# Two-layer hybrid transformer block on one core: the first norm's modulations as float32 matmuls, both conditions at once

## The chip, the cores and the metric

The kernel runs on one core of a Trainium2 chip. The metric is device time in microseconds (us) of one execution; the time of a kernel is the median of its runs.

A core has TensorE (in the profile PE, and PEld for its weight loads), VectorE (DVE), ScalarE (ACT), GpSimd (POOL), and SyncE (SP), whose queue issues most of the loads here. Each engine takes its own instructions in the order in which they were compiled. The "granted clock" is the share of TensorE's full clock that the chip allowed in a stretch of time.

## The reference

Two streams go through two layers: 512 latent tokens `x` and 256 context tokens `ctx`, each 1024 wide. In each layer a conditioning vector (`c` for the latents, `c_ctx` for the context) gives six vectors of 1024, the modulations. Cut to what matters here:

```python
def rms_norm(x, g):
    y = xf * lax.rsqrt(jnp.mean(xf * xf, axis=-1, keepdims=True) + EPS)
    return y * g

def adaln(cond, w_mod, b_mod):
    return jnp.split(jax.nn.silu(cond) @ w_mod + b_mod, N_MOD, axis=-1)

for l in range(DEPTH):
    sh1, sc1, gt1, sh2, sc2, gt2 = adaln(c, w_mod[l], b_mod[l])
    csh1, csc1, cgt1, csh2, csc2, cgt2 = adaln(c_ctx, w_mod[l], b_mod[l])
    h_ctx = rms_norm(ctx, norm1[l]) * (1 + csc1) + csh1
    h = rms_norm(x, norm1[l]) * (1 + sc1) + sh1
    p = h @ w_in[l]          # q, k, v, the convolution branch, the spatial gate, three gates
    ...                      # attention, two other branches, merge, output projection
    x = x + gt1 * merged
    x = x + gt2 * swiglu(rms_norm(x, norm2[l]) * (1 + sc2) + sh2)
```

The change concerns `sh1`, `sc1`, `csh1` and `csc1` of layer 0: 2048 columns of `w_mod[0]` (1024 rows each), multiplied with two vectors.

## The kernel before

**Layout and arithmetic.** Activations lie with the feature on the partition: eight column tiles (k = 0 to 7) of 128 features by 768 tokens, 512 latent ones and then 256 of the context. A matrix product splits each operand into two float32r parts, a high part (ScalarE casts, line 201) and the rest (GpSimd or VectorE subtracts, line 202), and makes three passes on TensorE per 128x128 weight tile (line 211): high by high, high weights by low activations, low weights by high activations. `load_piece` (189) brings in 128x512 weights (tiles `ws`, five buffers) and splits them (`wh`, `wl`, four buffers each).

**Modulations.** `mod_block` (126) makes one 128-feature block of one modulation on VectorE. It loads the block transposed (two halves of 128x512, tiles `wm`, six buffers, line 130), multiplies each half with the Silu of the conditioning vector, which lies broadcast over the partitions in `sbc`, and sums along the row (line 136). Line 139 adds the bias, and line 143 makes `G1`, the norm's gain times one plus the scale. In layer 0 the first norm needs 16 blocks (eight of the scale, eight of the shift).

**The beginning.** The conditioning vector, x in three loads and the first weights are brought in. `norm_stats` (223) sums the squares, reduces them over partitions with float32 matmuls against a column of ones (235), and leaves the reciprocal root in a PSUM tile `RB`. Then, for each column tile k, line 408 on: two `mod_block`s for the latents' condition, `norm_apply` (248: VectorE line 254, ScalarE 256 or 259, and the split into `hh` and `hl`), and 18 passes on TensorE (six weight tiles of `w_six`, three passes each) that add to six open PSUM banks: the latents' k, v and four q projections. `first_stage` (317) lets the first six `wm` loads wait for a copy by GpSimd that reads x.

**After it.** The second condition is loaded to `sbc` (417). `post_k`, `post_v` and `post_q` work on the six banks (head statistics with float32 matmuls at line 295, and a rotation by 32 partitions through DMAs on ScalarE's queue, `rope`, 389). Then come the latents' convolution branch (`branch_a`, 454) and spatial gate (`branch_c`, 492). Amid these steps `ctx_mods` (558) makes the same 16 blocks again, for the context's condition, with the weights read again. After all of them comes the context's norm (568), and then the context's projections, attention, merge, output projection and feed forward. The other modulations are made later by the same `mod_block`, both conditions at once, a block at a time beside the merge and the feed forward (`pump`).

**What sets the order.** The code gives an order in which the program is written; a planner then simulates the engines and places each instruction on its engine when its operands are there, earlier instructions of the program first. Buffers are handed out by the same planner: an instruction that needs a buffer waits for the last reader of its former content. Some loads are held back by hand, with a one-element GpSimd copy into the tile that reads a later activation (lines 322, 416, 420, 426).

Of the kernel before, what the change touches and what calls it, by code (L numbers as in the profile page):

```python
# [16 lines left out]
P = 128  # L17
# [3 lines left out]
KD = 8  # L21
# [3 lines left out]
# columns of the packed small vectors, per layer  # L25
# [7 lines left out]
NPRE = 1  # merge columns whose gates are computed while the attention runs  # L33
# [3 lines left out]
def dit_block(ctx: ExitStack, tc: tile.TileContext, xT, conds, vecs, ident_in, rope_c, rope_s,  # L37
# [5 lines left out]
    PBUFS = {"D": 4, "F": 1, "O": 1, "PT": 2, "st": 1, "RB": 1, "hst": 1, "KB": 1, "VT": 1, "gst": 1,  # L43
# [27 lines left out]
    # four of the eight banks stay with two wide tiles, which the scores and the products take in turn  # L71
# [3 lines left out]
    def banks(n, tag):  # L75
        """n banks for the product of one block."""
        if tag != "D":
            return [pst(tag) for _ in range(n)]
        turn[0] += 1
        if n == 2:  # L80
            i = turn[0] % 3
            return [wide[i][:, 0:512], wide[i][:, 512:1024]] if i < 2 else [pst("D"), pst("D")]
        i = turn[0] % 8
        return [pst("D")] if i % 2 else [wide[i // 4][:, i // 2 % 2 * 512:i // 2 % 2 * 512 + 512]]

    def f(t):
        return t.bitcast(F32)

# [1 line left out]
    # one tile for all that stays  # L90
    fixed = const.tile([P, 3328], F32, name="fixed")
# [12 lines left out]
    sbc = keep(2, 1024)  # L104
    ident = keep(P)
# [49 lines left out]
    def wm_stage():  # L155
        return wp.tile([P, 512], F32, tag="wm", name="wm", bufs=6)
# [47 lines left out]
    def mm(dst, w, acts, segs, k=None):  # L204
        """dst[i][n, tok] (+)= sum_k w[k]^T act[k] for the segments, three passes of the split operands."""
        n = len(acts)
        for kk in ([k] if k is not None else range(n)):
            (wh, wl), (ah, al) = w[0 if k is not None else kk], acts[kk]
            for i, (ww, aa) in enumerate(((wh, ah), (wh, al), (wl, ah))):
                for d, (a, b) in zip(dst, segs):  # L210
                    nc.tensor.matmul(d[:, :b - a], lhsT=ww, rhs=aa[:, a:b], start=kk == 0 and i == 0,  # L211
                                     stop=kk == n - 1 and i == 2)
# [59 lines left out]
    def lagged(gemm_j, full, parts, norm_of, nlag=4):  # L272
        """the first columns whole; the last ones part by part, the norm of one part under the next."""
# [34 lines left out]
    nc.scalar.dma_start(sbc[:, 0, :], conds[0:1, :].to_broadcast([P, 1024]))  # L308
# [5 lines left out]
    nc.scalar.activation(sbc[:, 0, :], sbc[:, 0, :], AF.Silu)  # L314
    n_stage = [0]

    def first_stage():
        """the first of these loads go after most of x."""
        t = wm_stage()
        n_stage[0] += 1  # L320
        if n_stage[0] <= 6:
            nc.gpsimd.tensor_copy(t[:, 0:1], X[NX][:, 0:1])
        return t

    for l in range(2):
# [5 lines left out]
        # ================= tiles of the attention =================  # L331
# [57 lines left out]
        def rope(t):  # L389
            """rotates the latent columns of t in place."""  # L390
# [12 lines left out]
        # ================= norm 1, the first projections =================  # L403
        h = hnext if last else new_h()
        if l == 0:
            six = [wide[0][:, 0:512], wide[0][:, 512:], wide[1][:, 0:512], wide[1][:, 512:], pst("D"), pst("D")]
# [15 lines left out]

        late = h[0 if last else 3][0]  # loads that are not needed at once wait for this
# [26 lines left out]
        # ================= branch a: gated short convolution =================  # L450
# [33 lines left out]
        # ================= branch c: spatial gate =================  # L484
# [66 lines left out]
        def run(*gens):  # L551
            """takes a step of each in turn."""
# [25 lines left out]
        # ================= attention =================  # L578
# [77 lines left out]
        # ================= gated merge =================  # L656
# [44 lines left out]
        # ================= output projection and residual =================  # L701
# [25 lines left out]
        # ================= feed forward =================  # L727
# [49 lines left out]
def _layout(inp):  # L777
    """Host side: layout only (transposes, reorders, copies)."""
# [16 lines left out]
    for l in range(2):  # L795
# [12 lines left out]

    w_modT = a["w_mod"].transpose(0, 2, 1).reshape(2, 48, P, 1024)
# [5 lines left out]
        "xT": xT, "conds": np.stack([a["c"][0], a["c_ctx"]]), "vecs": vecs, "ident": np.eye(P, dtype=f4), "rope_c": rope_c, "rope_s": rope_s,  # L815
# [21 lines left out]
```

## Time and profile before

| | |
|---|---|
| median of 3 runs | 2028.22 us (2025.04 to 2030.04) |
| profiled execution, first to last instruction | 2027.8 us |
| mean granted clock | 0.984 |
| VectorE busy | 1061.6 us (52%) |
| ScalarE, GpSimd busy | 709.3 us (35%), 816.6 us (40%) |
| all bytes read from the chip's memory | 213.53 MB |

The profile lists each engine's instructions with their start and length. In a row such as `L211 PE MATMUL wide<-hh,wh 128*128 128x512 f32`, L211 is the code line, then come engine, operation, the tile written and those read, and the shapes. A row of a timeline begins with the start and the length in us; in brackets behind it stands how long the engine had been idle and what ended that. "SPq" and "ACTq" are issues of DMAs. In a table by stretches each row is a stretch of the execution, its length, and for each engine busy us and number of instructions, then the granted clock, the busy share of the 16 DMA engines and GB/s. Matmuls overlap, so a matmul's length is longer than the distance of two starts; the distance is what counts in a chain. A float32 matmul shows as two load-and-matmul pairs.

### The profile page before, as it was taken

The numbers are of one execution on the slowest core, as the hardware profiler recorded it, in microseconds if no ns is written. First come the engines' busy times: TensorE is split into PE (matmuls) and PEld (weight loads), VectorE is DVE, ScalarE is ACT, GpSimd is POOL, SyncE is SP. The second block draws the span as 40 slices with busy tenths as digits, with TensorE's granted clock in tenths as the row PEclk, the third lists the DMA queues.
The fourth block names the chain that finished last, engine by engine and source line by source line (L and its number), as shares of the span: only waits on it lengthen the run. The fifth ranks groups of instructions, "written<-read, shape, count | busy, mean of one in ns | idle before, by whom it ended". The sixth has DMA issues, their size and how long they took to land.

```text
span 2027.8 us, 28580 instructions
## 1 busy us (share of the span) xinstructions
PE 1931.9 (95%) x10390; PEld 1653.6 (82%) x10390; DVE 1061.6 (52%) x2104; ACT 709.3 (35%) x1361; POOL 816.6 (40%) x702
## 2 busy tenths in 40 slices
PE   5789999998899999999999999999999999999999
PEld 4578998887788788888888888787878888888887
DVE  7977775999999722212221236648733362222222
ACT  3336765212123422212202225447633353223231
POOL 5567644646322422212312226753333343323232
PEclk9899999999899999999999999999999999999999
DMA  8833211545579221221121124330032343333332
GB/s 290 271 109 99 69 32 60 185 151 165 172 244 337 89 63 47 63 79 49 56 89 48 46 73 150 104 104 11 17 104 89 120 135 104 100 98 93 100 100 87
DMA packets 124445, 223.27 MB, mean 110 GB/s; under 512 B 14224, under 2 KB 23184, under 8 KB 124304
## 3 DMA queue, kind: packets, MB, share of 16 engines
q1 hardware_dynamic: 122240, 218.30, 34.1%
q10 hardware_dynamic: 2064, 3.15, 0.5%
q8 instruction: 82, 1.34, 0.3%
q14 instruction: 59, 0.48, 0.1%
HBM read 213.53 MB, written 5.24 MB: 108 GB/s over the span
## 4 chain that ended last, share of the span: by engine, by line
PE 61%; DVE 5%; issue 1%; ACT 1%; DMA 0%; POOL 0%; ACTq 0%; DVEq 0%; POOLq 0%
PE wide L211 34%; PE pD L211 24%; PE pF L211 1%; PE pO L626 1%; DVE junk L136 1%; DVE nm L597 1%; PE pPT L620 1%; DVE nacc L232 0%; PE wide L593 0%; DVE ptl L623 0%; DVE ny L254 0%; ACT pth L622 0%; DVE xr L717 0%; DVE wl L202 0%; DVE qq L398 0%
## 5 line engine op out<-in xcount | busy, mean ns | idle before, releaser
L202 POOL TENSOR_TENSOR wl<-ws,wh 128x512 fp32r<-128x512 f32 (+1 forms) x368 | 497.4, 1358 | 737.2 <-ACT wh L201 540.7
L201 ACT CAST wh<-ws 128x512 fp32r<-128x512 f32 (+1 forms) x560 | 328.3, 608 | 400.0 <-PE wide L211 99.3
L211 PE MATMUL wide<-hh,wh 128*128 128x512 f32 (+1 forms) x1264 | 390.9, 361 | 26.9 <-ACT gate L663 10.1
L211 PE MATMUL wide<-hl,wh 128*128 128x512 f32 (+1 forms) x1264 | 393.9, 362 | 4.3 <-POOL hl L202 3.5
L211 PE MATMUL wide<-hh,wl 128*128 128x512 f32 (+1 forms) x1264 | 389.9, 359 | 2.2 <-POOL wl L202 1.5
L202 DVE TENSOR_TENSOR wl<-ws,wh 128x512 fp32r<-128x512 f32 x192 | 181.7, 946 | 313.3 <-ACT wh L201 290.5
L211 PEld LDWEIGHTS wide<-hh,wh 128*128 128x128 f32 x1264 | 213.6, 192 | 65.8 <-ACT gate L663 11.5
L136 DVE SCALAR_TENSOR_TENSOR junk<-wm,fixed 128x512 f32<-128x512 f32 x320 | 258.5, 818 | 6.7 <-DMA wm<-in_w_modT 4.7
L211 PEld LDWEIGHTS wide<-hl,wh 128*128 128x128 f32 x1264 | 215.0, 192 | 42.0 <-POOL hl L202 5.4
L211 PEld LDWEIGHTS wide<-hh,wl 128*128 128x128 f32 x1264 | 215.2, 192 | 39.4 <-POOL wl L202 1.9
L211 PE MATMUL pD<-hh,wh 128*128 128x512 f32 (+1 forms) x632 | 209.2, 364 | 4.3 <-DVE qq L379 1.5
L211 PE MATMUL pD<-hl,wh 128*128 128x512 f32 (+1 forms) x632 | 212.0, 365 | 0.6 <-POOL hl L202 0.5
L211 PE MATMUL pD<-hh,wl 128*128 128x512 f32 (+1 forms) x632 | 210.4, 363 | 1.7 <-POOL wl L202 1.7
L202 POOL TENSOR_TENSOR ul<-su,uh 128x768 fp32r<-128x768 f32 (+1 forms) x44 | 69.4, 1577 | 199.8 <-ACT uh L201 192.5
L211 PEld LDWEIGHTS pD<-hh,wh 128*128 128x128 f32 x632 | 111.5, 190 | 23.7 <-ACT qa L383 1.9
L211 PEld LDWEIGHTS pD<-hh,wl 128*128 128x128 f32 x632 | 112.6, 190 | 21.7 <-POOL wl L202 2.3
L211 PEld LDWEIGHTS pD<-hl,wh 128*128 128x128 f32 x632 | 112.1, 190 | 19.7 <-POOL hl L202 1.2
L201 ACT CAST uh<-su 128x768 fp32r<-128x768 f32 (+1 forms) x44 | 32.0, 728 | 224.5 <-DVE su L740 224.5
L602 POOL TENSOR_SCALAR pp<-pp,nm 128x768 f32<-128x768 f32 (+1 forms) x80 | 66.9, 838 | 97.8 <-DVE nm L601 67.4
L211 PE MATMUL wide<-ul,wh 128*128 128x512 f32 (+1 forms) x310 | 94.5, 356 | 0.0
L211 PE MATMUL wide<-uh,wl 128*128 128x512 f32 (+1 forms) x310 | 93.6, 352 | 0.0
L211 PE MATMUL wide<-uh,wh 128*128 128x512 f32 (+1 forms) x310 | 93.4, 352 | 0.0
(238 smaller groups left out, 3155.3 us busy)
## 6 DMA issues: line engine op xcount, KB each, us to landing
ws<-in_w SPq DMA_DIRECT2D x244, 256.0 KB, 2.7
wm<-in_w_modT SPq DMA_DIRECT2D x224, 256.0 KB, 4.0
ws<-in_w_in SPq DMA_DIRECT2D x184, 256.0 KB, 3.0
ws<-in_w_o SPq DMA_DIRECT2D x48, 256.0 KB, 4.0
ws<-in_w_abc SPq DMA_DIRECT2D x32, 256.0 KB, 2.8
ws<-in_w SPq DMA_DIRECT2D x36, 192.0 KB, 2.5
ws<-in_w_six SPq DMA_DIRECT2D x16, 192.0 KB, 4.8
xr<-in_xT SPq DMA_DIRECT2D x8, 384.0 KB, 6.4
```

Source lines behind the costliest of these rows:

```text
L136: nc.vector.scalar_tensor_tensor(junk, parts[hh], 1.0, sbc[:, c, hh * 512:(hh + 1) * 512], op0=ALU.mult, op1=ALU.mult, accum_out=acc[:, hh ...
L201: nc.scalar.copy(hi, src)
L202: (lo_eng or nc.gpsimd).tensor_tensor(lo, src, f(hi), op=ALU.subtract)
L211: nc.tensor.matmul(d[:, :b - a], lhsT=ww, rhs=aa[:, a:b], start=kk == 0 and i == 0, stop=kk == n - 1 and i == 2)
L597: nc.vector.tensor_reduce(nm[:, 0:1], D[:, :nk], axis=AX.X, op=ALU.max, negate=True)
L602: nc.gpsimd.tensor_scalar(pt[:, :nk], pt[:, :nk], nm[:, 3:4], 0.0, op0=ALU.mult, op1=ALU.add)
L620: nc.tensor.transpose(TD[:, (2 * j + cc) * P:(2 * j + cc + 1) * P], pts[cc][:, kc:kc + P], ident)
L626: nc.tensor.matmul(o[:, 0:256], lhsT=v3[:, kt, :], rhs=pp[:, j * 256:(j + 1) * 256], start=gi == 0 and j == 0 and i == 0, stop=gi == len(k ...
```

## The change

- The host lays out the scale and shift columns of `w_mod[0]` as `w_m0`, untransposed, with 128x128 blocks that TensorE can take as weights, and both conditions as `condT` (128 partitions, 8 by 2). The kernel loads `condT` first and takes its Silu (16 columns).
- `first_loads(b)` brings in the four 128x512 pieces for column tile b (new tiles `wmt`, 14 buffers). `first_mods(b)` makes scale and shift of both conditions with 16 float32 matmuls of two columns into a new PSUM tile `md`, and VectorE writes `G1` and `MOD` from it with two small operations. `bm1` holds the scale's bias plus one.
- In the loop over k the loads and matmuls of k + 1 stand ahead of the passes of k. The two pieces of `w_six` are loaded together.
- `first_stage`, the latents' 16 `mod_block`s, `ctx_mods` and its loads go. The context's norm takes its steps amid the latents' branches.
- The broadcast conditions in `sbc`, which the later modulations still read, are loaded on ScalarE's queue after the last column's `hh`, and their Silu stands before the attention.

```diff
+    sct = keep(KD, 2)
+    nc.sync.dma_start(sct, condT)
...
-    nc.scalar.dma_start(sbc[:, 0, :], conds[0:1, :].to_broadcast([P, 1024]))
...
-    nc.scalar.activation(sbc[:, 0, :], sbc[:, 0, :], AF.Silu)
-    n_stage = [0]
-
-    def first_stage():
...
+    nc.scalar.activation(sct, sct, AF.Silu)
+    bm1 = keep(KD)
+    nc.vector.tensor_scalar(bm1, vcol(0, V_BM + KD, KD), 1.0, None, op0=ALU.add)
+
+    def first_loads(b):
+
+        parts = []
+        for i in range(2):
+            for hh in range(2):
+                t = wp.tile([P, 512], F32, tag="wmt", name="wmt", bufs=14)
+                nc.sync.dma_start(t, w_m0[b, i][:, 4 * hh:4 * hh + 4, :].rearrange("p k n -> p (k n)"))
+                parts.append(t)
+        return parts
+
+    def first_mods(b, parts):
+        md = pst("md")
+        for i in range(2):
+            for k in range(KD):
+                nc.tensor.matmul(md[:, 2 * i:2 * i + 2], lhsT=parts[2 * i + k // 4][:, k % 4 * P:k % 4 * P + P],
+                                 rhs=sct[:, k, :], start=k == 0, stop=k == KD - 1)
+        nc.vector.tensor_scalar(G1[0][:, b, :], md[:, 0:2], bm1[:, b:b + 1], vcol(0, V_N1 + b),
+                                op0=ALU.add, op1=ALU.mult)
+        nc.vector.tensor_scalar(MOD[0][:, 0, b, :], md[:, 2:4], vcol(0, V_BM + b), None, op0=ALU.add)
...
+            first_mods(0, first_loads(0))
             RB = norm_stats(X, *XS)
+            six += [pst("D"), pst("D")]
             for k in range(KD):
-                for sec in (1, 0):
-                    mod_block(0, sec, k, (0,), first_stage)
+                if k < KD - 1:
+                    mparts = first_loads(k + 1)
                 norm_apply(X, RB, G1[0], MOD[0][:, 0], k, *XS, h[k])
+                w = []
                 for hb in range(2):
-                    w = load_piece(w_six[k][:, hb * 384:(hb + 1) * 384])
-                    for b in range(3):
-                        mm([six[3 * hb + b]], w[b:b + 1], h, [XS], k=k)
-            nc.gpsimd.tensor_copy(sbc[:, 1, 0:1], f(h[0][0][:, 0:1]))
-            nc.sync.dma_start(sbc[:, 1, :], conds[1:2, :].to_broadcast([P, 1024]))
-            nc.scalar.activation(sbc[:, 1, :], sbc[:, 1, :], AF.Silu)
+                    w += load_piece(w_six[k][:, hb * 384:(hb + 1) * 384])
+                if k < KD - 1:
+                    first_mods(k + 1, mparts)
+                for b in range(6):
+                    mm([six[b]], w[b:b + 1], h, [XS], k=k)
...
+            for c in range(2):
+                nc.gpsimd.tensor_copy(sbc[:, c, 0:1], f(h[7][0][:, 0:1]))
+                nc.scalar.dma_start(sbc[:, c, :], conds[c:c + 1, :].to_broadcast([P, 1024]))
...
-            def ctx_mods():
-                for k in range(KD):
-                    for sec in (1, 0):
-                        mod_block(0, sec, k, (1,), wm_stage)
-                    yield
-
             def small_x():
                 yield from branch_a(*XS, "D")
                 yield from branch_c(*XS, "D")
-            run(ctx_mods(), small_x())
-            for _ in norm(X, G1[0], MOD[0][:, 0], *CS, h):
-                pass
+            run(small_x(), norm(X, G1[0], MOD[0][:, 0], *CS, h))
...
+        if l == 0:
+            for c in range(2):
+                nc.scalar.activation(sbc[:, c, :], sbc[:, c, :], AF.Silu)
         preload(AF.Exp, br["c", 1][0][:, W - 1:W])
```

More of the change, by code (lines that the diff above doesn't have):

```diff
@@ L36, in dit_block @@
 @with_exitstack
-def dit_block(ctx: ExitStack, tc: tile.TileContext, xT, conds, vecs, ident_in, rope_c, rope_s,
+def dit_block(ctx: ExitStack, tc: tile.TileContext, xT, conds, condT, w_m0, vecs, ident_in, rope_c, rope_s,
               w_modT, w_six, w_in, w_abc, w_o, w_13, w_2, ws_t, bs, out):
@@ L42, in dit_block @@
     big = ctx.enter_context(tc.tile_pool(name="big", bufs=1))
[L43 removed]
+    PBUFS = {"D": 4, "F": 1, "O": 1, "PT": 2, "st": 1, "RB": 1, "hst": 1, "md": 1, "KB": 1, "VT": 1, "gst": 1,
              "gT": 2, "mix": 2}
@@ L87, in f @@
         return t.bitcast(F32)
-    fixed = const.tile([P, 3328], F32, name="fixed")
+    fixed = const.tile([P, 3360], F32, name="fixed")
     used = [0]
@@ L405, in dit_block @@
         if l == 0:
-            six = [wide[0][:, 0:512], wide[0][:, 512:], wide[1][:, 0:512], wide[1][:, 512:], pst("D"), pst("D")]
+            six = [wide[0][:, 0:512], wide[0][:, 512:], wide[1][:, 0:512], wide[1][:, 512:]]
+            first_mods(0, first_loads(0))
             RB = norm_stats(X, *XS)
+            six += [pst("D"), pst("D")]
             for k in range(KD):
-                for sec in (1, 0):
-                    mod_block(0, sec, k, (0,), first_stage)
+                if k < KD - 1:
+                    mparts = first_loads(k + 1)
                 norm_apply(X, RB, G1[0], MOD[0][:, 0], k, *XS, h[k])
+                w = []
                 for hb in range(2):
-                    w = load_piece(w_six[k][:, hb * 384:(hb + 1) * 384])
-                    for b in range(3):
-                        mm([six[3 * hb + b]], w[b:b + 1], h, [XS], k=k)
-            nc.gpsimd.tensor_copy(sbc[:, 1, 0:1], f(h[0][0][:, 0:1]))
-            nc.sync.dma_start(sbc[:, 1, :], conds[1:2, :].to_broadcast([P, 1024]))
-            nc.scalar.activation(sbc[:, 1, :], sbc[:, 1, :], AF.Silu)
+                    w += load_piece(w_six[k][:, hb * 384:(hb + 1) * 384])
[3 more added lines that the diff above has]
+                    mm([six[b]], w[b:b + 1], h, [XS], k=k)
             for k in range(KD):
```

9 lines of the change are left out of this document (3 added, 6 removed).

## The prediction

> **What bounds the kernel now.** I read the page first, then the stretch sums (windows), then the timeline of the stretches that the change touches.
>
> ```profile
> span 2027.8 us, 28580 instructions
> ...
> PE 1931.9 (95%) x10390; PEld 1653.6 (82%) x10390; DVE 1061.6 (52%) x2104; ACT 709.3 (35%) x1361; POOL 816.6 (40%) x702
> ...
> PE   5789999998899999999999999999999999999999
> ...
> DVE  7977775999999722212221236648733362222222
> ...
> PEclk9899999999899999999999999999999999999999
> DMA  8833211545579221221121124330032343333332
> ```
>
> TensorE sets the end: 95% of the span, and nearly all slices at 9. Only the first three slices of 51 us are below 9, with the transfers at 8 in the first two. The change acts there, so I cut that part by what happens: up to the first projection matmul (25.39), the six projections (to 67.70), the latents' branches (to 160), and a stretch of the same kind with no modulation work (to 260). Columns: length, then busy us and count for PE, PEld, DVE, ACT, POOL, then granted clock, DMA share, GB/s.
>
> ```profile
> 0.00:25.39 25.39, 2.98 (x12) 2.49 (x12) 14.59 (x35) 11.08 (x17) 9.14 (x15) 1.00 0.88 294
> 25.39:67.70 42.31, 37.28 (x144) 28.00 (x144) 40.45 (x94) 17.62 (x35) 26.86 (x31) 1.00 0.87 276
> 67.70:160.00 92.30, 75.92 (x333) 61.17 (x334) 77.86 (x145) 34.16 (x62) 56.57 (x40) 0.89 0.53 164
> 160.00:260.00 100.00, 95.93 (x721) 91.58 (x720) 75.19 (x161) 71.15 (x150) 73.27 (x66) 0.97 0.28 85
> ```
>
> The same stretches, the dot products of the modulations (L136) alone; columns DVE busy, clock, DMA share, GB/s:
>
> ```profile
> 25.39:67.70 42.31, 24.50 (x56) 1.00 0.87 276
> 67.70:160.00 92.30, 28.18 (x58) 0.89 0.53 164
> ```
>
> VectorE is full (40.45 of 42.31) during the six projections, 24.50 of it L136. After 67.70 L136 takes another 28.18, for the context. TensorE idles 92.30 - 75.92 = 16.4 us there, and its clock is 0.89.
>
> **What goes.** Both passes of L136 with their small operations, that is 52.7 us of VectorE after 25.39, half of the 16.8 MB read for them (64 loads of 256 KB by the code), and the waits that they cause. The largest of these waits after 67.70, and a stretch of SP's queue of loads:
>
> ```profile
> L211 PE MATMUL wide<-hh,wh 128*128 128x512 f32 (+1 forms) x43 | 20.2, 469 | 7.5 <-DVE az L463 2.6 <-DVE acv L474 2.4 <-ACT wh L201 1.8
> L211 PE MATMUL pD<-hh,wh 128*128 128x512 f32 (+1 forms) x42 | 16.4, 390 | 2.9 <-DVE qq L379 1.5 <-DVE hms L297 1.4
> ```
>
> ```profile
> 83.86 10.92 SPq L130 DMA_DIRECT2D wm<-in_w_modT x9
> 95.41 0.33 SPq L194 DMA_DIRECT2D ws<-in_w_in  x1
> ```
>
> VectorE operations that free banks (az, acv, qq, hms) end 7.9 us of TensorE's idle time. On SP's queue nine modulation loads spread over 10.92 us hold up the next weight load. The clock is lost with the gaps:
>
> ```profile
> 71.30:81.54 10.24, 8.10 (x23) 6.14 (x23) 9.35 (x26) 2.98 (x6) 4.88 (x4) 0.50 0.94 309
> 95.19:102.02 6.83, 5.36 (x13) 4.20 (x14) 6.80 (x12) 2.19 (x4) 6.83 (x5) 0.50 0.78 254
> 136.15:139.56 3.41, 3.41 (x10) 2.63 (x9) 1.11 (x2) 3.29 (x6) 3.41 (x4) 0.50 0.51 165
> ```
>
> TensorE is busy 8.10 + 5.36 + 3.41 = 16.9 us at half clock, which loses half, 8.4 us. So 16.4 + 8.4 = 24.8 us are lost from 67.70 to 160. Not all comes back: from 160 to 260, with no modulations, 4.1 us are idle, and a clock of 0.97 says that 6 us at half rate cost 3 more. The 67 us of work at 7 in 100 keep 5, and filling the weight buffers at the stage's begin takes about 1. I book **-19** (bounds -14 and -24).
>
> **What comes.** Eight blocks (one per column tile) of 16 float32 matmuls, 128x128 weights by 2 columns. The nearest rows are the head statistics at full clock and the norm statistics at half clock, with single passes of the projections, warm and cold, beside them:
>
> ```profile
> 16.25 1.87 PE L235 MATMUL pst<-fixed,nacc 128*128 128x1 f32 x8 [16.25 <-DVE nacc L232]
> ...
> 28.98 0.63 PE L211 MATMUL wide<-hh,wl 128*128 128x512 f32 x1
> 29.40 0.63 PE L211 MATMUL wide<-hl,wh 128*128 128x512 f32 x1
> ...
> 47.72 0.39 PE L211 MATMUL wide<-hh,wl 128*128 128x512 f32 x1
> 47.95 0.40 PE L211 MATMUL wide<-hh,wh 128*128 128x512 f32 x1
> ...
> 69.12 1.03 PE L295 MATMUL phst<-fixed,hsq 128*128 128x2 f32 x8
> ```
>
> L295's row holds 4 matmuls of the code in 8 instructions. Less a tail of about 0.25 us, 1.03 us over 7 steps are 0.111 a step, 0.223 a matmul; L235's 1.87, less 0.35, are 0.214 a step at half clock, 0.43 a matmul. A 512-column pass starts 0.23 after the one before it (warm), 0.42 (cold). So a matmul for two columns costs as much as a whole pass: 128 x 0.223 = 28.5 us on the engine that sets the end, 55 if cold. This can't be hidden except before the first projection matmul, where TensorE has 2.98 us of work in 25.39.
>
> How much fits there? x has landed at 10.9, where the copies that wait for it start, and the first pass of a projection comes at 25.40:
>
> ```profile
> 10.90 1.76 POOL L322 COPY wm<-xin 128x1 f32<-128x1 f32 x6 [10.48 <-DMA xin<-in_xT]
> ```
>
> ```profile
> 25.40 1.22 PE L211 MATMUL wide<-hh,wh 128*128 128x512 f32 x2 [2.42 <-ACT hh L201]
> ```
>
> At 294 GB/s the first block's 1.05 MB follow x in 3.6 us, its first quarter by 11.8. 16 cold matmuls take 6.8: 18.6. The norm's statistics stand behind them on TensorE: 1.7 more, 20.3, where they ended at 18.1 before. From their end to 25.40 the norm's chain took 7.3 us; with some cold float32 matmuls ahead of its transposes 1.5 more. The first pass starts at **29** instead of 25.4, and some 18 more matmuls have run: 34 of 128. Left from 29 on: 144 x 0.227 = 32.7 and 94 x 0.223 = 21.0, together 53.7. The start at half clock (28.98 and 29.40 still show it 4 us after the first pass) loses some 2.4: 85.1. The rest hides under TensorE's 7.6 us a column (18 passes and 16 float32 matmuls): of the 40.45, 17.62 and 26.86 us of VectorE, ScalarE and GpSimd for eight columns VectorE loses over half and the others nothing, so the largest, GpSimd, has 3.4 a column; and a column's loads, 1.44 MB, take 5.0 us with 3.5 columns of them ahead. The two small operations that read a block's bank stand on the same cover.
>
> Then the clock. Four windows of one length (columns as in the stretches), then the float32 matmuls of L235 alone in the third (PE, PEld). The first window holds passes only:
>
> ```profile
> 54.23:57.64 3.41, 1.72 (x8) 1.13 (x7) 3.30 (x10) 1.83 (x5) 1.68 (x3) 1.00 0.82 256
> 57.64:61.05 3.41, 2.77 (x12) 1.92 (x12) 3.41 (x7) 1.99 (x6) 2.72 (x3) 1.00 0.87 292
> 661.80:665.21 3.41, 2.19 (x19) 1.99 (x18) 2.84 (x7) 1.66 (x3) 0.45 (x1) 1.00 0.33 102
> 665.21:668.62 3.41, 3.41 (x18) 3.41 (x17) 2.28 (x6) 2.40 (x6) 2.31 (x3) 0.50 0.12 26
> ```
>
> ```profile
> 661.80:665.21 3.41, 0.77 (x7) 0.78 (x7) 1.00 0.33 102
> ```
>
> After 1.72 us of passes in a window the clock stays; after 2.19 us, of which 0.77 are float32 matmuls with one column and 1.42 passes, it is halved. So such matmuls don't count as work for the clock, or for little. A block of 16 takes 3.6 us, a little more than a window; the clock falls in some 4 of the 5 blocks that stand between dense groups, and a drop costs about one window at half rate, 1.7 us: **6.8** (bounds 0 and 5 x 3.4 = 17). The six projections end at 92, not 67.7: **+24**.
>
> By the Trainium skill ("TensorE: Matmul & The Clock Gate", section "Why this matters for your kernels") what costs the clock in mid-kernel is an idle gap of more than about 3 us between matmul bursts, and these blocks leave no such gap. By that rule the sum would be the first rival's; the row at 661.80 speaks against it, with no gap of that length and half the clock behind it.
>
> Smaller edits cost nothing on the path, because the covering engines have room (ScalarE 34.16 of 92.30, GpSimd 56.57): two row loads of the conditions on ScalarE's queue, each behind a GpSimd copy that waits for the last hidden column (weight casts queue behind them; without cover up to 2 us once), two Silu over 1024 columns moved to before the attention, up to two table loads, the context's norm moved earlier. Gone are the six gate copies (1.76).
>
> Sum: +24 - 19 = +5 on 2027.8, and the shown median (2028.22) lies 0.4 above this execution: **2033**. A measurement of this kernel tells about 0.3%, 6 us, from no change, so this is "same" with a lean to slower.
>
> **Rivals.**
> 1. The float32 matmuls count for the clock. It is then up from about 18: 42 are done by 26.5, and the projections end near 79.5: +12 - 19 = -7, **2021**. For it: no row has a long chain of them. Against: 661.80. Chance 0.15. (This is where the Trainium skill's page "TensorE: Matmul & The Clock Gate", named above, leads.)
> 2. The planner mixes blocks and passes finely while the clock is up. Passes are then half of every window, as at 54.23, and no drop comes: 85 - 67.7 - 19 = -2, **2026**. For it: the passes of a column are already taken out of order as operands come. Against: a block's operands are there early, and whole groups are ready. Chance 0.16.
> 3. The same fine mix while the clock is down, from 29 on: passes then carry 0.23 in every 0.85 us, a smaller share than the 1.42 in 3.41 after which it fell at 661.80, and nothing wakes it. All 238 run at 0.427: end at 131, +63 - 19 = +44, **2071**. It decides where groups become shorter than two windows of cold passes. Chance 0.06.
> 4. The waits from 67.70 on have another cause: ScalarE's casts and the rotation's transfers. Only 9 come back: **2043**. For it: 1.8 of the idle time is laid to casts. Against: VectorE is 84% busy there. Chance 0.13.
>
> **How the numbers follow.** The forecast has 0.50; its own range is 2021 to 2049 (+17.4 to 67.70 without drops, drops 0 to 17, -14 to -24 after). Range over all: 2016 to 2050, which leaves out rival 3 and half of the far ends. Faster by over 0.3% (under 2022): half of rival 1 and shares of the forecast and of rival 2, 0.23. Slower (over 2034): near half of the forecast, rivals 3 and 4, 0.38. The rest 0.39.
>
> **What would show it.** Six projections end at 87 to 100, with five or so half-clock windows between 30 and 92; float32 matmuls 0.22 us apart warm; after the projections a clock near 1, TensorE idle under 6 us in the next 70, VectorE near half busy. A first pass before 26, no half-clock windows, or an end of the projections before 82 would show my path wrong; so would idle time as long as before behind them.

## The result and the profile after

| | before | after |
|---|---|---|
| median, same chip | 2027.99 us (4 runs, 2025.04 to 2030.04) | 2039.66 us (4 runs, 2039.11 to 2040.96) |
| ratio | | 1.0062, 95% interval 1.0048 to 1.0076 |
| profiled execution, first to last instruction | 2027.8 us | 2036.9 us |
| all bytes read from the chip's memory | 213.53 MB | 205.15 MB |

The changed kernel is slower by 11.7 us. The forecast was 2033, range 2016 to 2050. Its lines are numbered two higher up to 297 (the passes are now L213), and the new matmuls are L333. From the page of the changed kernel:

```profile
span 2036.9 us, 28706 instructions
...
PE 1971.9 (97%) x10646; PEld 1692.2 (83%) x10646; DVE 979.3 (48%) x1945; ACT 705.9 (35%) x1362; POOL 805.1 (40%) x697
...
PE   8989999989899999999999999999999999999999
...
PEclk9899999989999999999999999999999999999999
```

VectorE lost 82 us and TensorE gained 40 busy us and 256 instructions (128 float32 matmuls of two each). The hole in TensorE's first three slices is nearly closed, and the kernel is slower all the same: what fills the hole is work that wasn't there before.

The same stretches as in the prediction: to the first pass, to the end of the six projections, to the point that before had reached at 160 (found by matching the matmuls of both traces), and 100 us more. Columns: length, busy us and count for PE, PEld, DVE, ACT, POOL, granted clock, DMA share, GB/s.

```profile
0.00:30.13 30.13, 21.35 (x101) 21.33 (x101) 10.07 (x22) 12.09 (x20) 8.65 (x12) 1.00 0.98 359
30.13:92.67 62.54, 62.54 (x317) 54.17 (x318) 12.39 (x31) 18.07 (x34) 21.87 (x33) 0.86 0.43 135
92.67:167.80 75.13, 67.84 (x330) 56.59 (x329) 46.02 (x65) 35.80 (x66) 54.60 (x40) 0.95 0.29 88
167.80:267.80 100.00, 94.23 (x718) 89.75 (x718) 77.39 (x157) 69.29 (x144) 71.88 (x66) 0.98 0.26 84
```

The projections end at 92.67 instead of 67.70: +25.0. The next stage takes 75.13 instead of 92.30 for the same TensorE work (330 and 333 records): 17.2 come back. The delay is then 7.8, and the following 100 us hold as many matmuls as before (718 and 721), so it stays there. During the projections TensorE has changed places with VectorE: it is busy in all of 62.54, VectorE in 12.39.

Of that, the float32 matmuls alone (PE, PEld):

```profile
0.00:30.13 30.13, 19.04 (x88) 19.12 (x88) 1.00 0.98 359
30.13:92.67 62.54, 20.64 (x169) 21.38 (x169) 0.86 0.43 135
```

88 instructions, 44 of the 128 matmuls, are done before the first pass. TensorE's timeline shows at what rate:

```profile
8.78 7.09 PE L333 MATMUL pmd<-fixed,wmt 128*128 128x2 f32 x32 [8.78 <-ACT fixed L315]
...
17.44 6.11 PE L333 MATMUL pmd<-fixed,wmt 128*128 128x2 f32 x28
...
24.30 5.97 PE L333 MATMUL pmd<-fixed,wmt 128*128 128x2 f32 x28
30.13 1.20 PE L213 MATMUL wide<-hh,wh 128*128 128x512 f32 x2
...
34.54 0.59 PE L213 MATMUL wide<-hl,wh 128*128 128x512 f32 x1
34.97 0.40 PE L213 MATMUL wide<-hh,wl 128*128 128x512 f32 x1
...
41.59 3.63 PE L333 MATMUL pmd<-fixed,wmt 128*128 128x2 f32 x32
```

Ahead of 30.13, 28 instructions take 5.97 to 6.11, 0.21 each: half clock, after 20 us in which TensorE had hardly paused. (The clock column says 1.00 in that stretch. Passes 0.43 apart after 30.13, under the same 1.00, show that the column is no guide before its first recorded change; the distance of the starts is.) Only 4.8 us after the first pass, at 34.97, do the passes change from 0.43 to 0.23 apart, and the block at 41.59 takes 3.63 for 32, 0.11 each. In the kernel before, with only 2.98 us of work on TensorE ahead of its first pass, that change came 4.9 us behind it too (25.40 to 30.26).

Then the clock falls four times before the projections end. The windows ahead of and in three of the drops, and the last drop:

```profile
41.79:45.20 3.41, 3.41 (x32) 3.41 (x32) 0.00 (x0) 0.00 (x0) 1.37 (x2) 1.00 0.87 271
45.20:48.61 3.41, 3.41 (x10) 2.64 (x10) 1.87 (x4) 1.53 (x3) 1.42 (x5) 0.50 0.50 167
52.03:55.44 3.41, 3.41 (x27) 3.22 (x28) 0.93 (x3) 0.62 (x1) 1.27 (x1) 1.00 0.60 172
55.44:58.85 3.41, 3.41 (x10) 2.64 (x9) 0.14 (x1) 2.06 (x4) 1.97 (x2) 0.50 0.34 116
69.09:72.51 3.42, 3.42 (x27) 3.23 (x27) 0.97 (x3) 0.00 (x0) 0.94 (x1) 1.00 0.81 235
72.51:75.92 3.41, 3.41 (x10) 2.66 (x9) 0.16 (x1) 2.17 (x4) 1.71 (x2) 0.50 0.01 2
79.33:86.16 6.83, 6.83 (x24) 5.96 (x24) 1.82 (x4) 1.34 (x2) 1.10 (x3) 0.50 0.17 51
```

In the three windows ahead of a drop TensorE is busy throughout. The passes (L213) alone in these windows, then in three others: two behind which the clock stays, and the one ahead of the last drop:

```profile
41.79:45.20 3.41, 0.12 (x1) 0.15 (x2) 1.00 0.87 271
52.03:55.44 3.41, 1.10 (x5) 0.94 (x6) 1.00 0.60 172
69.09:72.51 3.42, 1.15 (x5) 0.99 (x6) 1.00 0.81 235
```

```profile
58.85:62.27 3.42, 1.47 (x7) 0.87 (x5) 1.00 0.74 200
62.27:65.68 3.41, 2.04 (x9) 1.70 (x10) 1.00 0.77 240
75.92:79.33 3.41, 1.42 (x6) 0.82 (x5) 1.00 0.14 55
```

Ahead of the four drops stand 0.12 to 1.42 us of passes; the rest of these windows is float32 matmuls. With 1.47 us the clock stays. The row at 661.80 that the prediction reads (1.42 us of passes, there of 256 columns, and the clock fell) fits that. The border isn't sharp: in the first experiment's kernel a window with 1.36 us holds (70.90) and one with 1.57 doesn't (521.50). The four drops hold 3.41 + 3.41 + 3.41 + 6.83 = 17.1 us at half rate, some 8.5 lost.

The length of the steps agrees with the Trainium skill ("TensorE: Matmul & The Clock Gate", section "What's actually happening": a free-running window of 3413 ns). Its rule in "Why this matters for your kernels", that in mid-kernel an idle gap of over about 3 us costs the clock, doesn't cover these drops: there was no gap at all.

Behind the projections one wait stands out in the changed kernel (us, times, longest):

```profile
PE phst L297 <- DVE acv L492: 4.3, 1, 4.3
```

and the clock is at 0.50 once, from 123.70 to 130.53; before it was there three times, for 20.5 us.

### The profile page after: what moved, and what is told of

Its sections match the earlier page's. It is cut to its first block, busy times and chain, and to the rows that moved or that the text cites. A ratio compares the mean times of both kernels' runs of the same rounds, so it can differ in the third digit from the quotient of the medians.

```text
span 2036.9 us, 28706 instructions
## 1 busy us (share of the span) xinstructions
PE 1971.9 (97%) x10646; PEld 1692.2 (83%) x10646; DVE 979.3 (48%) x1945; ACT 705.9 (35%) x1362; POOL 805.1 (40%) x697
## 3 DMA queue, kind: packets, MB, share of 16 engines
HBM read 205.15 MB, written 5.24 MB: 103 GB/s over the span
## 4 chain that ended last, share of the span: by engine, by line
PE 63%; DVE 11%; issue 2%; DMA 2%; ACT 1%; POOL 0%; ACTq 0%; SPq 0%; DVEq 0%; POOLq 0%
PE wide L213 35%; PE pD L213 24%; DVE junk L138 5%; DVE fixed L141 1%; PE pO L639 1%; PE pF L213 1%; DMA wm<-in_w_modT 1%; PE pPT L633 1%; DVE nm L610 1%; DVE wl L204 1%; DVE gate L682 0%; PE wide L606 0%; DVE ny L256 0%; DVE nacc L234 0%; DMA xr<-in_xT 0%
## 5 line engine op out<-in xcount | busy, mean ns | idle before, releaser
L204 POOL TENSOR_TENSOR wl<-ws,wh 128x512 fp32r<-128x512 f32 (+1 forms) x368 | 494.9, 1350 | 788.0 <-ACT wh L203 415.3
L203 ACT CAST wh<-ws 128x512 fp32r<-128x512 f32 (+1 forms) x560 | 323.5, 608 | 328.9 <-DVE junk L138 72.1
L213 PE MATMUL wide<-hh,wh 128*128 128x512 f32 (+1 forms) x1264 | 392.8, 362 | 16.5 <-ACT gate L676 10.3
L213 PE MATMUL wide<-hl,wh 128*128 128x512 f32 (+1 forms) x1264 | 392.9, 361 | 1.4 <-POOL hl L204 1.1
L213 PE MATMUL wide<-hh,wl 128*128 128x512 f32 (+1 forms) x1264 | 393.3, 361 | 0.8 <-DVE wl L204 0.8
L204 DVE TENSOR_TENSOR wl<-ws,wh 128x512 fp32r<-128x512 f32 x192 | 167.6, 873 | 389.3 <-ACT wh L203 177.0
L213 PEld LDWEIGHTS wide<-hh,wh 128*128 128x128 f32 x1264 | 215.3, 193 | 55.1 <-ACT gate L676 11.6
L213 PEld LDWEIGHTS wide<-hl,wh 128*128 128x128 f32 x1264 | 214.8, 192 | 38.7 <-POOL hl L204 1.7
L213 PEld LDWEIGHTS wide<-hh,wl 128*128 128x128 f32 x1264 | 215.2, 192 | 37.1 <-DVE wl L204 1.2
L213 PE MATMUL pD<-hh,wl 128*128 128x512 f32 (+1 forms) x632 | 212.6, 366 | 0.6 <-POOL wl L204 0.6
L213 PE MATMUL pD<-hh,wh 128*128 128x512 f32 (+1 forms) x632 | 211.7, 366 | 1.4 <-ACT hh L203 1.4
L213 PE MATMUL pD<-hl,wh 128*128 128x512 f32 (+1 forms) x632 | 212.2, 365 | 0.6 <-POOL hl L204 0.5
L138 DVE SCALAR_TENSOR_TENSOR junk<-wm,fixed 128x512 f32<-128x512 f32 x256 | 194.0, 771 | 4.8 <-DMA wm<-in_w_modT 4.8
L213 PEld LDWEIGHTS pD<-hh,wh 128*128 128x128 f32 x632 | 112.8, 191 | 21.6 <-ACT hh L203 1.6
L213 PEld LDWEIGHTS pD<-hl,wh 128*128 128x128 f32 x632 | 112.7, 191 | 20.9 <-POOL hl L204 1.2
L213 PEld LDWEIGHTS pD<-hh,wl 128*128 128x128 f32 x632 | 112.3, 190 | 20.4 <-POOL wl L204 1.0
L213 PE MATMUL wide<-uh,wl 128*128 128x512 f32 (+1 forms) x310 | 93.9, 353 | 0.0
L213 PE MATMUL wide<-ul,wh 128*128 128x512 f32 (+1 forms) x310 | 93.7, 353 | 0.0
L213 PE MATMUL wide<-uh,wh 128*128 128x512 f32 (+1 forms) x310 | 93.6, 352 | 0.0
```

Of the source, the lines that this page charges most:

```text
L138: nc.vector.scalar_tensor_tensor(junk, parts[hh], 1.0, sbc[:, c, hh * 512:(hh + 1) * 512], op0=ALU.mult, op1=ALU.mult, accum_out=acc[:, hh ...
L203: nc.scalar.copy(hi, src)
L204: (lo_eng or nc.gpsimd).tensor_tensor(lo, src, f(hi), op=ALU.subtract)
```

## The experiments

Differences are to the median of the kernel before in the same set of runs on the same chip; that of the changed kernel is +11.7.

**What the matmuls cost.** Each sum runs over one row tile of eight only, so seven eighths of the arithmetic are left out:

```diff
-            for k in range(KD):
+            for k in range(1):
...
-                                 rhs=sct[:, k, :], start=k == 0, stop=k == KD - 1)
+                                 rhs=sct[:, k, :], start=k == 0, stop=True)
```

> Leaves out part of the computation: each scale and shift block of the first norm is summed over one of its eight row tiles only, so 16 of the 128 float32 matmuls are left; all loads, the moved context norm and the rest stay. Main theory (the 128 float32 matmuls, at the price of a pass each, and the clock that they lose are what the change costs): the six projections end near 64 to 68 instead of 92.4, no or one half-clock window between 35 and the end, and the whole is 22 to 28 us shorter than the changed kernel, so about 2014, ratio to before near 0.993. Rival (the loads of the new weights or the moved context norm hold TensorE up): the projections still end above 80, and the time stays above 2030.

Measured: 2007.65, ratio 0.9903 (0.9888 to 0.9917), -19.3, 31 us better than the change by the differences to before. To the first pass, and to the end of the projections:

```profile
0.00:21.17 21.17, 5.62 (x24) 5.31 (x25) 9.49 (x24) 9.57 (x16) 3.23 (x7) 1.00 0.95 342
21.17:59.44 38.27, 38.27 (x169) 31.70 (x170) 13.93 (x29) 17.12 (x36) 27.19 (x36) 1.00 0.83 284
```

The projections end 33.2 earlier than in the changed kernel: 9.0 up to the first pass and 24.3 behind it. That is more than was expected (an end of 64 to 68, and 22 to 28 us less in all): up to there the clock doesn't fall, and the norm's chain doesn't stand behind cold matmuls. The transfers are all in place, so what the change pays up to the end of the projections is the arithmetic on TensorE.

**Does the mixture decide the clock?** Three blocks ahead of the loop; the other five spread over columns 1 to 5, three matmuls behind every three passes, tied in that order:

```diff
...
-                if k < KD - 1:
-                    first_mods(k + 1, mparts)
+                mix = first_mods(k + 2, ahead[k + 2]) if 0 < k < KD - 2 else iter(())
+                ins = None
                 for b in range(6):
-                    mm([six[b]], w[b:b + 1], h, [XS], k=k)
+                    with tc.issue_after(ins) if ins is not None else ExitStack():
+                        mm([six[b]], w[b:b + 1], h, [XS], k=k)
+                    for _ in range(3):
+                        ins = next(mix, ins)
...
```

> The same work as the changed kernel; three blocks of float32 matmuls run before the first pass, the other five are spread three at a time behind every three passes of columns 1 to 5, so no window of the clock is without passes. Main theory (float32 matmuls don't count for the clock, passes do, and about 1.4 of 3.4 us of passes keep it): one wake-up near 35, then no half-clock window until the projections end, at 82 to 85 instead of 92.4; the whole 8 us shorter than the changed kernel, about 2031. Rival (the clock falls for another reason, such as the rate of weight loads): half-clock windows remain and the end of the projections stays at 90 or later. Second rival (the mix never lets the clock wake): all of it at half rate, end of the projections above 115.

Measured: 2032.15, ratio 1.0022 (1.0013 to 1.0032), +5.2: 6.5 better than the change. From the first pass to the end of the projections:

```profile
32.95:87.57 54.62, 54.28 (x309) 47.08 (x310) 12.55 (x30) 18.05 (x35) 22.79 (x33) 1.00 0.45 144
```

The same 128 matmuls, and no drop from the wake-up at 38.2 to the end. The passes alone, in the one of its windows that holds the least of them:

```profile
65.56:68.97 3.41, 2.14 (x8) 1.19 (x8) 1.00 0.86 244
```

With 2.14 us of passes and more in every window the clock stays up. The end comes 5.1 earlier, although the first pass is 2.8 later (three blocks ahead of it, all cold), and 2.6 later than the 85 at most that was expected. So the drops come neither from idle time nor from the work as such, which is the same, but from windows with too few passes. In these kernels few passes and many float32 matmuls go together; at 661.80 in the kernel before, 0.77 us of float32 matmuls with the same 1.42 us of passes were enough for a drop, which speaks for the passes as what counts.

**Where the remaining 4 us come from.** Compared by the same matmuls, the delay of the changed kernel doesn't stay at 7.8: it is 6.4 at 700, 0.3 at 1200, about -1 near 1350 and 9.1 at the end, in stages that the change doesn't touch. (The traces differ by 9.1, the medians by 11.7: the profiled execution of before lies at the upper end of its kernel's times, near 2030.) In the two feed forwards TensorE is busy throughout in both; what differs is how many matmuls fit into 100 us. Before, then after:

```profile
800.00:900.00 100.00, 100.00 (x568) 86.67 (x567) 20.29 (x30) 16.26 (x30) 19.86 (x14) 1.00 0.23 69
1700.00:1800.00 100.00, 100.00 (x443) 82.81 (x442) 25.44 (x32) 27.94 (x47) 31.61 (x25) 1.00 0.32 98
```

```profile
800.00:900.00 100.00, 100.00 (x577) 87.92 (x576) 21.12 (x32) 16.88 (x30) 19.96 (x14) 1.00 0.20 62
1700.00:1800.00 100.00, 100.00 (x433) 81.22 (x432) 22.44 (x31) 27.91 (x49) 30.81 (x25) 1.00 0.30 93
```

1.6% faster in layer 0's feed forward, 2.3% slower in layer 1's, at the same clock: 6 us gained, 10 lost. One thing of the change that can reach there is the tile of constants `fixed`: with `sct` and `bm1` in it, it has 3360 columns of four bytes where it had 3328, which moves the tiles laid out behind it by 128 bytes. The kernel before with the wider tile, and the changed kernel with the narrower:

```diff
-    fixed = const.tile([P, 3328], F32, name="fixed")
+    fixed = const.tile([P, 3360], F32, name="fixed")
```

> The kernel before with nothing changed but the width of the tile of constants, 3360 instead of 3328 columns, as the change made it (all later tiles lie elsewhere in SBUF). In the feed forward the 512-column passes follow each other at 236 ns in layer 0 and 227 ns in layer 1 before, at 232 and 232 after. Theory (the places of the tiles set this): this kernel shows spacings unlike those of before, near 232 in one or both layers, and a time that differs by up to 10 us in either direction. Rival (the changed instructions or their order set it): 236 and 227 as before, and the same time within 0.2%.

> The changed kernel with the tile of constants at 3328 columns, as it was before (it still holds all). Theory (places of tiles): spacings in the feed forward change from 232 and 232 ns, towards 236 in layer 0 and 227 in layer 1; the end moves by less than 10 us. Rival (the changed instructions or the new tiles set it): 232 and 232 as in the changed kernel, the same time within 0.2%.

Measured, before with 3360: 2030.19, ratio 1.0013 (1.0005 to 1.0022), +3.2. After with 3328: 2034.10, ratio 1.0030 (1.0018 to 1.0042), +7.2, that is 4.5 better than the change as it stands (by the intervals these differences are known to within 2 to 4 us). The rates, first of before with 3360, then of after with 3328:

```profile
800.00:900.00 100.00, 100.00 (x573) 87.25 (x572) 21.31 (x32) 16.90 (x30) 19.34 (x14) 1.00 0.23 70
1700.00:1800.00 100.00, 100.00 (x436) 81.55 (x435) 24.53 (x31) 27.31 (x46) 30.65 (x24) 1.00 0.30 96
```

```profile
800.00:900.00 100.00, 100.00 (x567) 86.73 (x567) 21.15 (x32) 16.88 (x30) 19.90 (x14) 1.00 0.19 58
1700.00:1800.00 100.00, 100.00 (x443) 82.81 (x442) 23.19 (x32) 27.04 (x48) 30.68 (x24) 1.00 0.30 95
```

The rates go with the columns and not with the change. All nine kernels here with 3328 columns have 567 or 568 matmuls and 442 or 443, the four with 3360 have 571 to 577 and 433 to 437. Is it the size, or the offset within 512 bytes? 3456 columns move all by 512 bytes:

```diff
-    fixed = const.tile([P, 3328], F32, name="fixed")
+    fixed = const.tile([P, 3456], F32, name="fixed")
```

> The kernel before with the tile of constants at 3456 columns, 512 bytes a partition more than the 3328 of before (the changed kernel's 3360 are 128 bytes more). So far every kernel with 3328 showed 227 ns between the passes of layer 1, every one with 3360 some 230 to 232. Theory A (the offset of the tiles within 512 bytes sets it): 236 ns in layer 0 and 227 in layer 1 as before, time within 0.15% of before. Theory B (any other place of the tiles does it): spacings unlike those of before, as with 3360.

Measured: 2026.93, ratio 0.9994 (0.9984 to 1.0003), -1.3, no change that can be told. Its rates are those of 3328:

```profile
800.00:900.00 100.00, 100.00 (x568) 86.67 (x567) 20.34 (x32) 15.61 (x28) 18.43 (x14) 1.00 0.22 71
1700.00:1800.00 100.00, 100.00 (x443) 82.81 (x442) 25.13 (x32) 28.43 (x48) 30.07 (x23) 1.00 0.31 98
```

So not every move of the tiles changes the rates: one by 128 bytes does, one by 512 doesn't, which fits an offset within 512 bytes. No other width was tried. Which tile's offset it is, and why the two layers answer in opposite directions, stays open.

**What the context's dot products cost before.** In the kernel before, the context takes over the latents' modulations by a copy (its own are left out); the second pass of dot products and its loads are gone:

```diff
-                    for sec in (1, 0):
-                        mod_block(0, sec, k, (1,), wm_stage)
+                    nc.vector.tensor_copy(G1[0][:, k, 1:2], G1[0][:, k, 0:1])
+                    nc.vector.tensor_copy(MOD[0][:, 0, k, 1:2], MOD[0][:, 0, k, 0:1])
```

> The kernel before, with the context's first norm of layer 0 left without modulations of its own (it copies the latents'), so that the second pass of dot products and its loads are gone and nothing else changes. Main theory (this VectorE work and the loads that wait for it cause most of TensorE's idle time and of the half clock from 67.7 to 160): projections end near 67.5 as before, 15 to 19 us gained by the 100th us of TensorE's work, time about 2009 to 2012, ratio 0.991 to 0.993. Rival (the waits come from ScalarE's casts and the rotation's transfers): at most 9 us gained, time above 2018.

Measured: 2002.36, ratio 0.9887 (0.9873 to 0.9900), -24.6, the largest difference to before. The projections end at 66.29. From there to the point that before had reached at 160:

```profile
66.29:140.72 74.43, 68.90 (x334) 56.59 (x333) 46.89 (x64) 34.10 (x61) 55.24 (x39) 0.98 0.32 103
```

The stage takes 74.43 instead of the 92.30 of before, 17.9 less, and the kernel is 19.3 ahead at that point. The rest of the 24.6 comes in later stages, which the edit doesn't touch; why isn't shown. The fourth rival, that most of the waits there have another cause, falls. Two things go at once there, VectorE's time and the loads on SP's queue. To part them, the context's 32 loads got fourteen tiles of their own, so that the first fourteen are issued early and hold up the weights behind them less:

```diff
...
+            def late_stage():
+                t = wp.tile([P, 512], F32, tag="wmc", name="wmc", bufs=14)
...
-                        mod_block(0, sec, k, (1,), wm_stage)
+                        mod_block(0, sec, k, (1,), late_stage)
```

> The kernel before; only the loads of the context's 16 modulation blocks get 14 buffers of their own (six shared ones before), held back until the sixth hidden column, so that SP's queue no longer waits for VectorE with weight loads behind it. The dot products stay. Leaving them out gave 24.6 us. Theory A (the queue behind the loads makes a large part of that): 6 to 15 us faster than before, 2012 to 2021. Theory B (VectorE itself, full of dot products, holds the banks and casts up): within 5 us of before, 2022 to 2032.

Measured: 2022.72, ratio 0.9977 (0.9967 to 0.9986), -4.7. That is within what theory B gives. The projections, and from there to the same point:

```profile
25.43:69.84 44.41, 38.21 (x144) 29.92 (x145) 43.51 (x98) 17.37 (x35) 33.76 (x46) 0.96 0.92 310
69.84:161.67 91.83, 77.17 (x334) 62.72 (x333) 72.70 (x145) 35.38 (x65) 57.19 (x40) 0.87 0.43 141
```

The projections pay 2.1 for the loads that now run beside them. SP's queue is through with the modulation loads at 88.6 instead of 110.6, but the stage behind the projections takes 91.83, hardly less than the 92.30 of before, and the kernel is not ahead at its end. So the place of the loads in the queue isn't what costs there. VectorE's dot products are what is left, by elimination alone: leaving them out with all loads kept wasn't tried. The 4.7 come behind that point; why isn't shown.

**The moved norm.** The context's norm amid the latents' branches, in the kernel before:

```diff
-            run(ctx_mods(), small_x())
-            for _ in norm(X, G1[0], MOD[0][:, 0], *CS, h):
-                pass
+            run(ctx_mods(), small_x(), norm(X, G1[0], MOD[0][:, 0], *CS, h))
```

> The kernel before with one part of the change alone: the context's norm is written amid the latents' branches, each column behind its context modulations. Main theory (the norm's place is off the path): the same time within 0.3%, between 2022 and 2032. Rival (an earlier norm fills VectorE or holds a PSUM bank): slower by 4 us or more; or faster by 4 us or more if the idle time near 150 to 166 was the norm's.

Measured: 2028.27, ratio 1.0007 (0.9998 to 1.0016). It does nothing that can be measured. (Here each column waits for its context modulations, which the changed kernel has early.)

**A better version.** The fine mixture with 3328 columns (two edits from above together; only the second is shown):

```diff
-    fixed = const.tile([P, 3360], F32, name="fixed")
+    fixed = const.tile([P, 3328], F32, name="fixed")
```

> The mixed kernel (three blocks ahead, five spread among the passes) with the tile of constants at 3328 columns. If the places of the tiles and the clock are independent terms, it gains both: the mixed kernel's 7.5 us and the narrow tile's 5.6 us against the changed kernel, about 2026.5, the same as before within 0.2%. Pass spacing 236 ns in layer 0 and 227 in layer 1. Rival (the two overlap): 2031 or more.

Measured: 2029.31, ratio 1.0018 (1.0009 to 1.0027), +2.3: 9.4 better than the change, and still behind before. The two gains, 6.5 and 4.5, add up but for 1.6, which the spread of the runs can make. Moving all of the sums to TensorE doesn't pay even without drops.

So part of them: the first three column tiles on TensorE, both conditions of the other five on VectorE from one load during the projections, with 3328 columns of constants.

```diff
...
+                if k >= NT_PE:
+                    for sec in (1, 0):
+                        mod_block(0, sec, k, (0, 1), first_stage)
...
```

> TensorE makes the modulations of the first three column tiles only, both conditions at once, which it has time for before the first pass; VectorE makes those of the other five by dot products, both conditions from one load, while the projections run; none is left for later; tile of constants 3328 columns. Main theory (TensorE's float32 matmuls cost only where they stand among passes, VectorE's dot products only where they hold TensorE up): first pass at 28 to 32, projections end at 66 to 75, no context modulations behind them, so 12 to 20 us faster than before, 2007 to 2015. Rival (VectorE, with 40 dot products for both conditions, now sets the end of the projections): they end at 80 or later, and the time is 2018 to 2030.

Measured: 2027.35, ratio 1.0003 (0.9994 to 1.0012), where 2007 to 2015 was expected. VectorE sets the end of the projections, as the rival had it (46.08 of 49.26):

```profile
33.28:82.54 49.26, 41.44 (x157) 31.34 (x158) 46.08 (x110) 15.15 (x32) 31.33 (x31) 0.93 0.49 158
```

Then the kernel before with only the first two column tiles on TensorE, ahead of the first pass, and the other six as they were, once for each condition:

```diff
...
+            for k in range(2):
+                first_mods(k, first_loads(k))
             RB = norm_stats(X, *XS)
...
-                for sec in (1, 0):
+                for sec in (1, 0) if k > 1 else ():
                     mod_block(0, sec, k, (0,), first_stage)
...
-                for k in range(KD):
+                for k in range(2, KD):
...
```

> The kernel before, but TensorE makes the modulations of the first two column tiles, both conditions at once, ahead of the first pass; the other six stay on VectorE as they were, the context's amid the branches. Tile of constants 3328 columns. Theory (float32 matmuls are free where TensorE has nothing else, and VectorE's work falls by a quarter): first pass at 25 to 29, projections end at 61 to 67, a quarter of the 24.6 us behind them gained, so 6 to 12 us faster than before, 2015 to 2021. Rival (the first pass is late by as much as the rest gains): 2022 to 2030.

Measured: 2021.66, ratio 0.9972 (0.9960 to 0.9983), -5.8, just short of the 6 to 12 that were expected, and it beats both kernels. Apart from the two kernels that leave work out it is the best time here, if only 1 us ahead of that with the early loads.

```profile
0.00:30.15 30.15, 16.64 (x76) 16.15 (x77) 14.78 (x45) 11.55 (x19) 7.13 (x15) 1.00 0.97 341
30.15:69.62 39.47, 36.69 (x144) 29.02 (x145) 38.98 (x83) 16.60 (x33) 30.03 (x31) 0.96 0.83 271
```

The 32 matmuls run cold but where TensorE was idle. The first pass comes 4.8 later and the end of the projections 1.9 later than before, both later than expected (25 to 29, 61 to 67), and the later stages have a quarter less of the context's dot products. With the fourteen early tiles of the context's loads added as well:

```diff
...
-                        mod_block(0, sec, k, (1,), wm_stage)
+                        mod_block(0, sec, k, (1,), late_stage)
...
```

> The kernel of the two columns with the 14 own buffers for the context's loads. Under theory A of the kernel with the loads ahead, its gain comes on top: 2005 to 2015; under theory B the same as the two columns alone within 5 us.

Measured: 2025.14, ratio 0.9991 (0.9983 to 1.0000), -2.3, as theory B has it. The two gains of 5.8 and 4.7 don't add. By the traces this kernel and the one without the early loads are alike at the point that before reached at 160 (both some 7 us ahead of it); the early loads gain nothing there, as above. The two part in later stages, between 500 and 700, which neither edit touches; why, no run tells.

## Why the prediction was right, and where it was off

1. **Float32 matmuls of two columns cost as much as a pass, and double at half clock: right.** 0.223 and 0.43 were read from the statistics' rows; the block at 41.59 gives 3.63 / 16 = 0.227, the cold ones 5.97 / 14 = 0.43.
2. **First pass at 29: 30.13.** By then 44 matmuls were done, not 34. The planner put most of a third block into the norm's chain. The two errors partly cancel: the first pass is 1.1 later, and ten matmuls fewer, 2.2 us, stand behind it.
3. **The clock drops: right in cause and nearly in size.** Booked were 4 drops of 1.7, 6.8; there were four, one of them two windows long, 8.5. The fine mixture shows the cause. The first rival falls by the changed kernel itself: the 44 cold matmuls didn't wake the clock, and by that rival the end would have been near 79.5. The second rival (the planner mixes finely by itself) didn't come; the mixture had to be forced, and the end was then 87.57 against the 85 that it was given.
4. **Projections end at 92, +24: 92.67, +25.0.**
5. **Return of 19 behind it: 17.2.** Of the 24.8 lost there before, 5 + 1 were kept back; idle time alone was 75.13 - 67.84 = 7.3, and one drop of 6.83 stayed. The idle time has a part that the prediction did not see, 4.3 us in one piece, behind VectorE's `acv` of the convolution branch; all 7.3 lie in the first 70 us, where the prediction's sign was under 6. The kernel before without the context's dot products gives back 17.9 in the same stage, so the 5 + 1 that were kept back are about right.
6. **"Smaller edits cost nothing on the path": this step failed.** The edits as such are covered, and the moved norm alone measured nothing. But the change makes the tile of constants 32 columns wider, and that costs 4.5 us by the changed kernel with 3328 columns (3.2 by the kernel before with 3360). The prediction had no such term. Without it the change is worth +7.2, where +5 was forecast: +25.0 - 17.2 = +7.8 in the traces.
7. **The link to the median was wrong, at no cost.** A time of a run lies above its span: the changed kernel's 2036.9 belongs to its run of 2039.11. By the same distance the span of 2027.8 belonged to a run near 2030, the highest of those shown, and not to one 0.4 below their median. Forecasting the median by the sum of +5 gives 2033 either way.

So the sign and the path were right; 2.8 of the missing 6.7 us lie in steps 4 and 5, and about 4 in step 6, as far as differences of 2 us can be told. The forecast itself was weak: its range was 34 us wide, and a kernel slower by over 6 us had a chance of 0.38, as much as no change.

## What to carry to other kernels

Moving small sums to the engine that sets the end pays only as far as that engine is idle: with the same width of constants two of eight column tiles gained 5.8 us here, all eight lost 7.2. Where TensorE must take matmuls with few columns amid its main work, spread them so that every clock window still holds enough full passes (here 2.14 us of passes in each 3.41 held the clock; with 1.42 and less it fell four times). And when a difference shows in stages that an edit doesn't touch, look at whether it moved the tiles in memory before explaining it by the edit.

## What the runs showed of the hardware

- TensorE can be busy in 3.41 of 3.41 us and have its clock halved in the next window, if most of it is float32 matmuls with two columns. With 0.12 to 1.42 us of passes in the window the clock fell four times, with 1.47 it stayed once, with 2.14 and more it stayed in every window of the fine mixture; where in between the border lies isn't settled (1.36 held and 1.57 didn't in the kernel with one row tile of eight). Whether the number of columns or the data type is the reason wasn't tried.
- Twenty us of such matmuls in a row don't raise the clock: the starts of their instructions stay 0.21 us apart, and the clock is up only 4.8 us after the first pass (4.9 in the kernel before, without them).
- The rate of passes at full clock depends on where the tiles lie: 442 or 443 matmuls in 100 us of layer 1's feed forward with 3328 or 3456 columns of constants, 433 to 437 with 3360; in layer 0's 567 or 568 and 571 to 577, the other way round. On the whole run it is worth 3 to 4.5 us of 2030, by the medians of two pairs of kernels.
